# A one-layer hybrid decoder step: the step from the mixers to the feed-forward part, the planner's figures and the rank of the convolutions

## The chip, the cores and the metric

One core of one Trainium2 chip runs the whole kernel. The metric is the device time of one execution in microseconds (us).

## The reference, cut to what matters

2048 prompt tokens and 8 single-token samples pass one decoder layer of width 1024, in fp32:

```python
def trunk_layer(x, ...):
    h = rmsnorm(x, norm_mix_g)
    z = h @ w_in                                   # 1024 -> 1536 columns
    attn_out = sink_attention(q, k, v, ...)        # 8 heads of 64, 2 K/V heads, window 128, ALiBi, sinks
    conv_out = conv_module(z[..., V_END:C_END])    # gated, depthwise over 31 rows, layer norm, silu: 256 channels
    ssm_out  = ssm_module(z[..., C_END:])          # diagonal S5 scan, 16 groups x 64 states, gelu, gate
    x = x + jnp.concatenate([attn_out, conv_out, ssm_out], -1) @ w_out
    hf = rmsnorm(x, norm_ffn_g)
    return x + (silu(hf @ w_ff_gate) * (hf @ w_ff_up)) @ w_ff_down    # 1024 -> 2816 -> 1024
y = rmsnorm(trunk_layer(x), norm_final_g)
```

The new K/V rows, convolution rows and scan states are outputs too.

## The kernel before

**Precision.** Each matrix operand is kept as a high part of the faster fp32r type and a low part (the rest), and a product is three matmuls: high by high, high by low, low by high. A weight or activation is "split" by ScalarE, which writes the high part, and VectorE or GpSimd, which writes the low part by a subtraction.

**The planner.** Nearly all of the program is written as generators (tasks) that `Flow` runs at build time. A task yields what it needs next: an engine, buffers by tag, events. `Flow.run` repeatedly looks for the task that could begin first by an estimated clock for each engine, takes the tasks of the same engine that could begin within `SLACK` ns of it, and issues the piece of the one with the lowest priority number. What comes out is a fixed order of instructions for each engine and for the one DMA queue (SyncE's); on the chip each engine goes through its own order and waits by semaphores. The durations are those of `Engine.cost` (a function of the operation and of its columns), and `Flow.dma`. They are never run: they only choose the order. All instructions carry line 222 (the helper `planned`) and all DMAs line 163, so a trace is read by tile names.

**The mixers (first part).** The tokens are four quarters (512, 512, 512, 520 columns). `w_stream` (priority 50) multiplies each by w_in; `ssm(q)` (1 + q), `conv(q)` (100 + q) and `attention(q)` with its blocks (about 9.5 + 8 q to 17 + 8 q) are the mixers. The convolution is 31 multiply-adds of VectorE over 2 x 512 columns, a step of two at a time between which the planner may place other work. `out_stream` (45) multiplies the mixers' result by w_out, adds the residual and stores x2, in eight units m for each quarter; after a quarter's last unit it forms the inverse norm (two ones-matmuls for quarter 3, a square root on ScalarE, a reciprocal on VectorE), `RS_LATE` = 8000 ns later.

**The feed-forward part (second part).** The columns are three groups g (2 x 344, 2 x 342, 2 x 342 columns), and the intermediate width eleven steps f. A gate or up matrix of a step is a 2 x 2 block product by Strassen's scheme in Winograd's form: seven products of blocks in place of eight. The weights' blocks are A11, S1, S2, A12, S4, S3, A22 (in the order of use, 12 matmuls each), where S1 to S4 are sums that group 0 forms (VectorE, tag `sw`), splits and stores, and that groups 1 and 2 load again. The activations' blocks are B11, T1, T2, B21, B22, T3, T4, in the same order of use. They are formed from x2 by `prep_raw` (stored to DRAM, `hraw`), and loaded and split by `prep_block` through `tx` tiles, of which there are two. For group 0 their split halves lie in the two `h` tiles that the projection uses before (B11, T1, T2 in the first that comes free, B21, T3, T4 in the second, which is free when the projection has ended) and in a tile of its own for B22. `matrix` collects the products in PSUM banks of tag `mm` (three): A11 (bank a), S1 (c), S2 (b), then A12 onto a, S4 onto c, S3 onto b, and A22 into a fourth use of the tag. A bank is freed when VectorE or ScalarE has read its result. PSUM has three more banks of tag `sc` and two of tag `tr`. `down(g)` multiplies the products by w_ff_down and VectorE adds them to eight accumulator tiles `xa`, loaded with x2 by `load_acc`; `final` transposes and normalizes them at the end of a group.

The seam is the place where `out_stream` ends and `gate_up(0)` begins.

Of the kernel before, what the change touches and what calls it, by code (L numbers as in the profile page):

```python
# [9 lines left out]
F32 = mybir.dt.float32  # L10
F32R = mybir.dt.float32r
BF16 = mybir.dt.bfloat16
AF = mybir.ActivationFunctionType
OP = mybir.AluOpType
# [14 lines left out]
W = [512, 512, 512, 520]  # L29
TILES = [[(0, 512)]] * 3 + [[(0, 256), (256, 264)]]  # L30
RS_LATE = 8000.0
C1 = 6.28125
C2 = 0.0019350051879882812
C3 = 3.0199159819567e-07
# [17 lines left out]
class Flow:  # L52
# [89 lines left out]
    def rel(self, tag):  # L142
        self.free[tag].append(self.cur["fin"])
        self.free[tag].sort()
# [31 lines left out]
class Engine:  # L176
# [8 lines left out]
    def cost(self, op, out, ins, args, kw):  # L185
        n = 1
        for d in out.shape[1:]:
            n *= d
        psum = any(x.space == PSUM for x in ins)
        if self.name == "PE":  # L190
            if op == "transpose":
                return max(54.0, args[1].shape[0] / 1.2 + 2.5)
            if ins[0].dtype == F32R:
                return max(123.0, n / 2.4 + 18.0)
            ns = max(215.0, n / 0.6 + 6.0)
            return ns / 2 + 1.0 if out.shape[0] <= 64 else ns
        if self.name == "ACT":
            table, ns = self.TABLE.get(args[2]), 0.0
            if table and table != self.table:
                self.table, ns = table, 1283.0  # L200
            extra = sum(isinstance(kw.get(x), bass.AP) for x in ("scale", "bias", "accum_out"))
            return ns + (51.0 if psum else 94.0) + 94.0 * extra + 0.833 * n
        if self.name == "POOL":
            return 146.0 + (0.85 if op in ("memset", "affine_select") else 2.1) * n
        cols = sum(x.free_size() == 1 for x in ins)
        fast = op in ("tensor_copy", "tensor_scalar") and not psum
        per = 6.25 if op == "reciprocal" else 0.52 if fast else 0.26 if op == "memset" else 1.042
        at, read = (out.tensor, out.offset), [(x.tensor, x.offset) for x in ins]
        dep = 127.0 if self.wrote in read or at in self.read else 0.0
        self.wrote, self.read = at, read  # L210
        return 67.0 + 61.0 * cols + per * n + dep
# [15 lines left out]
def hybrid_step(  # L227
# [9 lines left out]
    nc = tc.nc  # L237
    fl = Flow(nc)
    fl.BIAS = {"DVE": 0, "POOL": -500}
    fl.SLACK = {"PE": 100, "ACT": 150, "DVE": 0, "POOL": 150, "SP": 50}  # L240
    V, S = Engine(fl, "DVE", nc.vector), Engine(fl, "ACT", nc.scalar)
    G, E = Engine(fl, "POOL", nc.gpsimd), Engine(fl, "PE", nc.tensor)
    dma, rel = fl.dma, fl.rel
# [55 lines left out]
    def ps_tr():  # L299
        return psum.tile([P, 512], F32, tag="tr", name="tr", bufs=2)  # L300
# [306 lines left out]
    def conv(q):  # L607
        yield "acc"
        acc = cpool.tile([P, 2, 512], F32, tag="acc", name="acc", bufs=1)
        yield "DVE", cu_ev[q, 0], cu_ev[q, 1], halo_ev[q], small_ev  # L610
        cu = CU[q]
        for i in range(2):
            V.tensor_scalar(acc[:, i, :], cu[:, i, 0:512], taps[:, i, 0:1], fv[:, i:i + 1], op0=OP.mult, op1=OP.add)
        for t in range(1, TAPS):
            for i in range(2):
                V.scalar_tensor_tensor(acc[:, i, :], cu[:, i, t:t + 512], taps[:, i, t:t + 1], acc[:, i, :],
                                       op0=OP.mult, op1=OP.add)
            if t < TAPS - 1:
                yield "DVE"
        cu_done(q)  # L620
        fl.add(layer_norm_gate(acc, 512, q, 0, "acc"), 2.5)
# [647 lines left out]
    segX_ev = Ev(sum(2 * len(x_rows(q)) for q in range(4)))  # L1269
    segA_ev = Ev(4 + 1 + 1)  # L1270
    segB_ev = Ev(5 + 4 + 1 + 1 + 32 + 4)
    attn_ev = Ev(16)
    for q in range(4):
        for k in range(KT):

# [26 lines left out]
    fl.add(w_stream(plan), 50)  # L1302
    for q in range(4):
        fl.add(ssm(q), 1 + q)
        fl.add(conv(q), 100 + q)
    fl.add(conv_tail(), 8)
    fl.add(states_prompt(), 7.5)

# [328 lines left out]
    def out_stream():  # L1637
        for q in range(4):
            yield "stg", Mev[q]
            ssq = stg()  # L1640
            chain = Ev()
            chain.hit(0.0)
            boxes = []
            for m in range(KT):
                ev, box = Ev(), []
                boxes.append((ev, box))
            fl.add(residual(q, 0, *boxes[0]), -600)
            for m in range(KT):
                if m + 1 < KT:
                    fl.add(residual(q, m + 1, *boxes[m + 1]), -400)  # L1650
                st = {"n": nt[q], "chain": chain}
                chain = Ev()

                def evac(ps, c0, n, q=q, m=m, ev=boxes[m][0], box=boxes[m][1], st=st, ssq=ssq, nxt=chain):
                    yield "DVE", ev
                    x2 = box[0]
                    V.tensor_tensor(x2[:, c0:c0 + n], ps[:, :n], x2[:, c0:c0 + n], op=OP.add)
                    rel("mm")
                    st["n"] -= 1
                    if st["n"]:  # L1660
                        return
                    yield "SP"
                    dma(x2_d[m][:, 512 * q:512 * q + W[q]], x2[:, :W[q]])
                    x2_ev[q, m].hit(fl.now())
                    w = W[q]
                    if m == 0:
                        yield "ACT", st["chain"]
                        S.activation(ssq[:, :w], x2[:, :w], AF.Square)
                        rel("x2")
                        segB_ev.hit(fl.now())  # L1670
                    else:
                        yield "ACT", "stg"
                        sq = stg()
                        S.activation(sq[:, :w], x2[:, :w], AF.Square)
                        rel("x2")
                        segB_ev.hit(fl.now())
                        yield "POOL", st["chain"]
                        G.tensor_tensor(ssq[:, :w], ssq[:, :w], sq[:, :w], op=OP.add)
                        rel("stg")
                    nxt.hit(fl.now())  # L1680
                    if m == KT - 1:
                        yield "stg", fl.later(RS_LATE)
                        rs = stg()
                        for c0, n in TILES[q]:
                            yield "PE", "tr"
                            pm = ps_tr()
                            E.matmul(pm[:, :n], ones_c, ssq[:, c0:c0 + n], start=True, stop=True)
                            yield "ACT"
                            S.activation(rs[:, c0:c0 + n], pm[:, :n], AF.Sqrt, scale=256.0 / D, bias=eps)
                            rel("tr")  # L1690
                        rel("stg")
                        yield "DVE"
                        V.reciprocal(rs[:, :w], rs[:, :w])
                        yield "SP"
                        dma(rs_d[:, 512 * q:512 * q + w], rs[:, :w])
                        rel("stg")
                        rs_ev[q].hit(fl.now())
                yield from dense(outs[KT * q + m], M[q], TILES[q], evac, -500)
            rel("h")

# [88 lines left out]
    def prep_block(g, b):  # L1791

        n = GN[g]
        yield ("SP", "tx", raw_ev[g, b], *([prog[g - 1, NFP - 1]] if g else [hb_free[-1, b]]))
        t = tx_tile().rearrange("p (k c) -> p k c", k=4)[:, :, :n]
        dma(t, raw_d[g][:, RAW.index(b), :, :n])
        yield "ACT", hb_free[g - 1, b]
        hi, lo = HB[b][:, 0, :, :n], HB[b][:, 1, :, :n]
        S.activation(hi, t, AF.Copy)
        yield "DVE"  # L1800
        V.tensor_tensor(lo, t, hi.bitcast(F32), op=OP.subtract)
        rel("tx")
        HB_ev[g, b].hit(fl.now())


    SUMS = ["S1", "S2", "S4", "S3"]
# [127 lines left out]
    def matrix(g, f, kind, done):  # L1934
# [27 lines left out]
            V.tensor_tensor(t["p5"], t["p5"], t["u3"], op=OP.add)  # L1962
            fl.add(done(1, 1, t["p5"], "gs", False), -500)

        def c21(ps):
            yield "DVE", e["u3"]
            V.tensor_tensor(t["r"], ps[:, :n], t["u3"], op=OP.add)
            rel("mm")
            rel("stg")
            fl.add(done(1, 0, t["r"], "stg", False), -500)  # L1970

# [22 lines left out]
        rel("whl")  # L1994
        fl.add(plus_r("u3", b, "stg", True), -500)
        fl.add(c22(), -499)
        yield "PE", "mm", u.ready["A22"], HB_ev[g, "T4"]
        d = ps_mm()
        yield from part(d, n, u, "A22", g, "T4", True, f, kind)
        rel("whl")  # L2000
        fl.add(c21(d), -500)

    def gate_up(g):
        n = GN[g]
        for f in range(NFP):
            prog[g, f].hit(fl.now())
            gate, gate_ev = {}, {(i, j): Ev() for i in range(2) for j in range(2)}
# [109 lines left out]

    def load_acc(g, m):

        yield ("SP", "xa", *[x2_ev[q, m] for q in quarters(g)])  # L2120
        x = fpool.tile([P, 688], F32, tag="xa", name="xa", bufs=8)
        dma(x[:, :2 * GN[g]], x2_d[m][:, G0[g]:G0[g] + 2 * GN[g]])
        X[g, m] = x
        X_ev[g, m].hit(fl.now())
# [123 lines left out]
```

## Time and profile before

| | |
|---|---|
| median of 3 runs | 2186.06 us (2183.65 to 2190.08) |
| the profiled execution's own time | 2186.88 us |
| its span, first to last instruction | 2185.1 us |
| TensorE busy | 2091.2 us, 96% |
| VectorE, ScalarE, GpSimd busy | 1533.9, 853.7, 254.0 us |
| granted TensorE clock, mean | 0.987 of full speed |
| DMA | 457.9 MB, 210 GB/s over the span |

The profile is one execution. Engines are called PE (TensorE), DVE (VectorE), ACT (ScalarE), POOL (GpSimd) and SPq (the DMA queue of SyncE); PEld is the weight load, which overlaps PE. A matmul's end is modelled, so "busy" tells that TensorE had work, and not how fast it went.

### The profile page before, as it was taken

What the parts mean: (1) busy time and instruction counts of PE and PEld (TensorE: products, weight loads), DVE (VectorE), ACT (ScalarE), POOL (GpSimd) and SP (SyncE); (2) the same over time, 40 slices, a digit from 0 to 9 for tenths busy, and PEclk for the clock granted to TensorE, in tenths of its full rate; (3) what the DMA queues carried; (4) which work ended last, traced back from release to release, by engine and by line L of the source; (5) the groups of instructions that cost most, each with busy time, mean ns of one, the idle gap of its engine ahead of it and who ended that gap; (6) DMA issues with size and microseconds to landing.
All of it is one profiled execution on the core that took longest, in us unless ns stands there. A gap on an engine that the chain in (4) does not pass through costs nothing.

```text
span 2185.1 us, 35164 instructions
## 1 busy us (share of the span) xinstructions
PE 2091.2 (96%) x13326; PEld 1950.1 (89%) x13326; DVE 1533.9 (70%) x3052; ACT 853.7 (39%) x1682; POOL 254.0 (12%) x183
## 2 busy tenths in 40 slices
PE   8899999999998899999999999999999999999997
PEld 7676777877777899999999999999999999999997
DVE  5998889789954577777787766656656655555555
ACT  6216534777641443333333442222223522222223
POOL 3201110122121322221322000000000000000000
PEclk9999999999999999999999999999999999999998
DMA  8964666688789966655565586656647765554551
GB/s 271 306 226 148 220 200 213 205 234 257 233 296 322 315 228 208 200 202 172 188 217 198 185 267 224 199 166 216 205 145 247 226 202 159 179 164 148 181 158 52
DMA packets 350713, 457.90 MB, mean 210 GB/s; under 512 B 42453, under 2 KB 233760, under 8 KB 340304
## 3 DMA queue, kind: packets, MB, share of 16 engines
q1 hardware_dynamic: 350544, 455.66, 65.0%
q8 instruction: 105, 1.72, 0.3%
q14 instruction: 64, 0.52, 0.1%
HBM read 333.94 MB, written 122.32 MB: 209 GB/s over the span
## 4 chain that ended last, share of the span: by engine, by line
PE 54%; DMA 3%; DVE 2%; issue 1%; ACT 1%; POOL 1%; SPq 0%; DVEq 0%; ACTq 0%; POOLq 0%
PE mm L222 34%; PE sc L222 20%; DMA tx<-hraw 1%; DMA xa<-x 1%; DVE sw L222 1%; POOL whl L222 1%; PE tr L222 1%; ACT whl L222 0%; DMA whl<-sum 0%; ACT h L222 0%; DVE h L222 0%; DVE act L222 0%; DVE gs L222 0%; DVE xa L222 0%; DVE stg L222 0%
## 5 line engine op out<-in xcount | busy, mean ns | idle before, releaser
L222 PE MATMUL mm<-h,whl 128*128 128x342 f32 (+4 forms) x7296 | 1270.3, 330 | 32.9 <-DVE gs L222 8.3
L222 PEld LDWEIGHTS mm<-h,whl 128*128 128x128 f32 x7296 | 1150.2, 190 | 101.4 <-issue 16.7
L222 PE MATMUL sc<-act,whx 128*128 128x342 f32 (+1 forms) x3168 | 514.2, 320 | 5.1 <-DVE xa L222 3.5
L222 PEld LDWEIGHTS sc<-act,whx 128*128 128x128 f32 x3168 | 499.5, 189 | 7.1 <-DVE xa L222 5.1
L222 DVE TENSOR_TENSOR xa<-xa,sc 128x342 f32<-128x342 f32 (+1 forms) x528 | 265.7, 510 | 224.0 <-PE sc L222 211.9
L222 DVE SCALAR_TENSOR_TENSOR acc<-cu,taps,acc 128x512 f32<-128x512 f32 x240 | 173.1, 783 | 0.0
L222 POOL TENSOR_TENSOR whl<-sw,whl 128x512 fp32r<-128x512 f32 x88 | 122.9, 1407 | 331.4 <-ACT whl L222 303.6
L222 ACT ACTIVATE whx<-wraw 128x1024 fp32r<-128x1024 f32 x66 | 66.6, 1053 | 227.7 <-PE sc L222 226.2
L222 PE MATMUL mm<-hb,whl 128*128 128x342 f32 (+1 forms) x792 | 136.0, 320 | 0.0
L222 ACT ACTIVATE stg<-mm 128x342 f32<-128x342 f32 (+3 forms) x100 | 49.8, 498 | 215.9 <-PE mm L222 210.8
L222 PEld LDWEIGHTS mm<-hb,whl 128*128 128x128 f32 x792 | 126.8, 189 | 0.3 <-ACT gs L222 0.3
L222 ACT ACTIVATE whl<-wraw 128x512 fp32r<-128x512 f32 (+1 forms) x122 | 84.9, 696 | 68.2 <-PE mm L222 40.0
L222 DVE TENSOR_TENSOR stg<-mm,stg 128x342 f32<-128x342 f32 (+1 forms) x132 | 67.4, 511 | 48.7 <-PE mm L222 46.3
L222 DVE TENSOR_TENSOR whl<-wraw,whl 128x512 fp32r<-128x512 f32 x102 | 77.8, 763 | 32.8 <-ACT whl L222 32.4
L222 ACT ACTIVATE act<-gs 128x342 fp32r<-128x342 f32 (+1 forms) x99 | 48.1, 485 | 124.4 <-DVE gs L222 124.4
L222 ACT ACTIVATE s<-s,sst 128x256 f32<-128x256 f32 (+1 forms) x196 | 90.3, 488 | 13.3 <-DVE sst L222 13.3
L222 ACT ACTIVATE whl<-xraw 128x512 fp32r<-128x512 f32 x96 | 60.0, 625 | 75.8 <-PE mm L222 36.2
L222 DVE TENSOR_TENSOR whl<-xraw,whl 128x512 fp32r<-128x512 f32 x96 | 74.1, 777 | 14.8 <-ACT whl L222 14.8
L222 ACT ACTIVATE whl<-sw 128x512 fp32r<-128x512 f32 x88 | 52.8, 624 | 78.7 <-PE mm L222 44.7
L222 ACT ACT_TABLE_LOAD x64 | 82.1, 1283 | 3.2 <-issue 1.5
L222 DVE TENSOR_TENSOR whx<-wraw,whx 128x1024 fp32r<-128x1024 f32 x66 | 78.1, 1222 | 3.8 <-ACT whx L222 0.4
L222 DVE TENSOR_TENSOR gs<-mm,gs 128x342 f32<-128x342 f32 (+1 forms) x66 | 33.8, 512 | 61.2 <-PE mm L222 61.2
(232 smaller groups left out, 1854.9 us busy)
## 6 DMA issues: line engine op xcount, KB each, us to landing
whl<-sum SPq DMA_DIRECT2D x176, 512.0 KB
sum<-whl SPq DMA_DIRECT2D x88, 512.0 KB
wraw<-in_w_ff_down SPq DMA_DIRECT2D x66, 512.0 KB
whl<-hl_o SPq DMA_DIRECT2D x24, 1024.0 KB
wraw<-in_w_ff_up SPq DMA_DIRECT2D x44, 512.0 KB
xraw<-in_w_ff_gate SPq DMA_DIRECT2D x42, 512.0 KB
whl<-hl_q SPq DMA_DIRECT2D x12, 1024.0 KB
tx<-hraw SPq DMA_DIRECT2D x14, 684.0 KB
```

Of the source, the lines that this page charges most:

```text
L222: return call(*args, **kw)
```

## The change

The planner's costs: an fp32 matmul of 512 columns into half of the partitions counts 734 ns, a ScalarE operation of over 128 columns with a strided operand 1.7 ns a column, a scan on VectorE 2.2 ns a column. Slack is now 200 ns on VectorE and none on ScalarE and GpSimd. The convolutions' priority is 9 + 8 q, just before the attention of the same quarter. Quarter 3's inverse norm comes 60 us after the projection in place of 8, with both its matmuls ahead of both roots. `gate_up(0)` begins when `out_stream` has ended. Block T4 of group 0 is loaded by four DMAs into four of the five `gs` tiles (`prep_last`) and not through `tx`. A22's product takes a bank of tag `tr` or `mm`, whichever was freed longer ago by the planner's clock. `load_acc` waits for the start of f = 1 of its group.

```diff
-            return ns / 2 + 1.0 if out.shape[0] <= 64 else ns
+            if out.shape[0] <= 64:
+                return 734.0 if n >= 512 else ns / 2 + 1.0
+            return ns
...
-            return ns + (51.0 if psum else 94.0) + 94.0 * extra + 0.833 * n
+            apart = any(x.ap[-1][0] != 1 for x in (out, ins[0])) and n > 128
+            return ns + (51.0 if psum else 94.0) + 94.0 * extra + (1.7 if apart else 0.833) * n
...
-        per = 6.25 if op == "reciprocal" else 0.52 if fast else 0.26 if op == "memset" else 1.042
+        per = 6.25 if op == "reciprocal" else 2.2 if op == "tensor_tensor_scan" else 0.52 if fast else 0.26 if op == "memset" else 1.042
...
-    fl.SLACK = {"PE": 100, "ACT": 150, "DVE": 0, "POOL": 150, "SP": 50}
+    fl.SLACK = {"PE": 100, "ACT": 0, "DVE": 200, "POOL": 0, "SP": 50}
...
-        fl.add(conv(q), 100 + q)
+        fl.add(conv(q), 9 + 8 * q)
...
-                        yield "stg", fl.later(RS_LATE)
+                        yield "stg", fl.later(RS_LATE if q < 3 else RS_LAST)
                         rs = stg()
-                        for c0, n in TILES[q]:
-                            yield "PE", "tr"
-                            pm = ps_tr()
+                        yield ("PE",) + ("tr",) * len(TILES[q])
+                        pms = [ps_tr() for _ in TILES[q]]
+                        for (c0, n), pm in zip(TILES[q], pms):
                             E.matmul(pm[:, :n], ones_c, ssq[:, c0:c0 + n], start=True, stop=True)
-                            yield "ACT"
+                        yield "ACT"
+                        for (c0, n), pm in zip(TILES[q], pms):
                             S.activation(rs[:, c0:c0 + n], pm[:, :n], AF.Sqrt, scale=256.0 / D, bias=eps)
                             rel("tr")
...
             rel("h")
+        out_ev.hit(fl.now())
...
+        if g == 0 and b == "T4":
+            yield from prep_last(n)
+            return
...
+    def prep_last(n):
+
+        yield "SP", "gs", "gs", "gs", "gs", raw_ev[0, "T4"]
+        ts = [gs()[:, :n] for _ in range(4)]
+        for k in range(4):
+            dma(ts[k], raw_d[0][:, RAW.index("T4"), k, :n])
+        yield "ACT", hb_free[-1, "T4"]
+        for k in range(4):
+            S.activation(HB["T4"][:, 0, k, :n], ts[k], AF.Copy)
+        yield "DVE"
+        for k in range(4):
+            V.tensor_tensor(HB["T4"][:, 1, k, :n], ts[k], HB["T4"][:, 0, k, :n].bitcast(F32), op=OP.subtract)
+            rel("gs")
+        HB_ev[0, "T4"].hit(fl.now())
...
-        yield "PE", "mm", u.ready["A22"], HB_ev[g, "T4"]
-        d = ps_mm()
+        bank = min(("tr", "mm"), key=lambda x: fl.free[x][0] if fl.free[x] else 1e18)
+        yield "PE", bank, u.ready["A22"], HB_ev[g, "T4"]
+        d = ps_tr() if bank == "tr" else ps_mm()
...
     def gate_up(g):
         n = GN[g]
+        if g == 0:
+            yield out_ev
...
-        yield ("SP", "xa", *[x2_ev[q, m] for q in quarters(g)])
+        yield ("SP", "xa", prog[g, 1], *[x2_ev[q, m] for q in quarters(g)])
```

## Rows read from the trace of the kernel before

**Rows 1.** Busy time of each engine in stretches, then clock, DMA share, GB/s.
```profile
core 0: us, PE busy (x) PEld busy (x) DVE busy (x) ACT busy (x) POOL busy (x), PEclk, DMA share, GB/s
0.00:360.00 360.00, 326.60 (x2221) 261.01 (x2222) 303.71 (x667) 157.26 (x243) 58.49 (x46) 0.97 0.69 221
360.00:620.00 260.00, 248.47 (x1546) 197.96 (x1545) 231.40 (x695) 183.20 (x502) 45.88 (x30) 0.99 0.77 234
620.00:742.70 122.70, 114.99 (x699) 100.81 (x698) 61.28 (x79) 35.90 (x61) 28.12 (x21) 0.97 0.98 328
742.70:790.00 47.30, 34.49 (x180) 32.70 (x179) 34.07 (x39) 28.11 (x40) 16.86 (x10) 0.86 0.97 328
790.00:1215.00 425.00, 413.75 (x2601) 409.93 (x2600) 324.20 (x512) 150.33 (x275) 104.60 (x76) 1.00 0.59 192
...
1300.00:1650.00 350.00, 350.00 (x2232) 350.00 (x2231) 210.56 (x383) 93.44 (x173) 0.00 (x0) 1.00 0.62 194
```

**Rows 2.** TensorE's timeline in the seam; in brackets idle time before, and who ended it.
```profile
751.16 0.42 PE L222 MATMUL mm<-h,whl 128*128 128x344 f32 x1 [3.20 <-ACT h L222]
752.78 3.34 PE L222 MATMUL mm<-h,whl 128*128 128x344 f32 x11 [1.20 <-DVE h L222]
...
764.42 0.66 PE L222 MATMUL mm<-h,whl 128*128 128x344 f32 x1 [3.87 <-ACT h L222]
766.05 1.80 PE L222 MATMUL mm<-h,whl 128*128 128x344 f32 x5 [0.97 <-DVE h L222]
...
787.20 9.37 PE L222 MATMUL mm<-h,whl 128*128 128x344 f32 x48 [3.58 <-DVE gs L222]
```

**Rows 3.** The DMA queue's timeline in the seam: when loads are issued.
```profile
725.75 1.34 SPq L163 DMA_DIRECT2D tx<-hraw  x2
...
742.92 0.33 SPq L163 DMA_DIRECT2D tx<-hraw  x1
...
756.84 0.38 SPq L163 DMA_DIRECT2D tx<-hraw  x1
757.26 6.08 SPq L163 DMA_DIRECT2D xa<-x  x8
```

**Rows 4.** ScalarE's timeline in the seam.
```profile
765.43 1.28 ACT L222 ACT_TABLE_LOAD   x1
766.72 0.47 ACT L222 ACTIVATE stg<-tr,eps 128x256 f32<-128x256 f32 x1
```

**Rows 5.** ScalarE's groups in 742.7 to 790: busy time, mean ns.
```profile
L222 ACT ACT_TABLE_LOAD x5 | 6.4, 1283 | 0.1
```

**Rows 6.** TensorE's waits in 840 to 1215: in total, times, longest.
```profile
PE mm L222 <- DVE gs L222: 4.7, 4, 1.2
PE mm L222 <- ACT whl L222: 4.3, 6, 0.7
```

**Rows 7.** VectorE's timeline in the seam.
```profile
772.89 3.40 DVE L222 RECIPROCAL stg<-stg 128x520 f32<-128x520 f32 x1 [0.68 <-ACT stg L222]
...
786.64 0.50 DVE L222 TENSOR_TENSOR gs<-mm,gs 128x344 f32<-128x344 f32 x1
```

**Rows 8.** Stretches of 4 us in the seam, columns as in rows 1.
```profile
764.00:768.00 4.00, 2.61 (x7) 2.22 (x8) 2.44 (x2) 3.96 (x6) 3.03 (x2) 0.50 1.01 301
768.00:772.00 4.00, 4.00 (x20) 3.81 (x19) 2.50 (x4) 2.53 (x4) 0.35 (x1) 0.74 1.04 407
...
788.00:792.00 4.00, 4.00 (x20) 4.00 (x19) 3.50 (x7) 0.95 (x2) 0.00 (x0) 0.68 1.05 351
```

**Rows 9.** The chain of waits at the start of group 1.
```profile
1281.46 9.62 DMA xa<-x
```

**Rows 10.** VectorE's timeline: the last taps of quarter 3's convolution.
```profile
608.02 2.71 DVE L222 SCALAR_TENSOR_TENSOR acc<-cu,taps,acc 128x512 f32<-128x512 f32 x4
```

**Rows 11.** TensorE's timeline: the last attention product, and quarter 3's projection.
```profile
614.86 1.94 PE L222 MATMUL tr<-s,vt 128*64 128x512 f32 x8
...
689.55 0.95 PE L222 MATMUL mm<-h,whl 128*128 128x256 f32 x6
```

**Rows 12.** A stretch of the projection, columns as in rows 1.
```profile
630.00:640.00 10.00, 10.00 (x47) 8.11 (x46) 1.93 (x3) 1.74 (x3) 3.04 (x3) 1.00 1.01 323
```

More of the change, by code (lines that the diff above doesn't have):

```diff
@@ L31 @@
 RS_LATE = 8000.0
+RS_LAST = 60000.0
 C1 = 6.28125
@@ L1271, in hybrid_step @@
     segB_ev = Ev(5 + 4 + 1 + 1 + 32 + 4)
-    attn_ev = Ev(16)
+    attn_ev, out_ev = Ev(16), Ev()
     for q in range(4):
@@ L1963, in c22, with c21 @@
             fl.add(done(1, 1, t["p5"], "gs", False), -500)
-        def c21(ps):
+        def c21(ps, bank):
             yield "DVE", e["u3"]
             V.tensor_tensor(t["r"], ps[:, :n], t["u3"], op=OP.add)
-            rel("mm")
+            rel(bank)
             rel("stg")
@@ L1996, in matrix @@
         fl.add(c22(), -499)
-        yield "PE", "mm", u.ready["A22"], HB_ev[g, "T4"]
-        d = ps_mm()
+        bank = min(("tr", "mm"), key=lambda x: fl.free[x][0] if fl.free[x] else 1e18)
+        yield "PE", bank, u.ready["A22"], HB_ev[g, "T4"]
+        d = ps_tr() if bank == "tr" else ps_mm()
         yield from part(d, n, u, "A22", g, "T4", True, f, kind)
         rel("whl")
-        fl.add(c21(d), -500)
+        fl.add(c21(d, bank), -500)
     def gate_up(g):
         n = GN[g]
+        if g == 0:
+            yield out_ev
         for f in range(NFP):
```

## The prediction

> **What bounds the kernel now.** I read the stretches first [rows 1]: busy time of each engine by stage, to see which engine fills which stage. TensorE is the bound nearly everywhere. In groups 1 and 2 of the feed-forward part it is busy 350.00 of 350 us, so nothing there can be won. What is open is its idle time elsewhere: 33.4 us in 0 to 360 (360 less 326.60), 11.5 in 360 to 620, 7.7 in 620 to 742.7, 12.8 in the seam from 742.7 to 790 (where the granted clock is also down to 0.86), and 11.3 in the rest of group 0 (790 to 1215). In 0 to 620 VectorE is the close second: 303.7 of 360 and 231.4 of 260 us.
>
> Then TensorE's timeline in the seam [rows 2], whose brackets tell how long it stood and who let it go. The projection ends near 742.7; group 0's first matrix runs A11, S1 and S2 and stops. It waits for block B21 (3.20 + 1.20 us, the tail of it on VectorE), for block T4 (3.87 for ScalarE's high half, 0.97 for VectorE's low half), and 3.58 us before A11 of f = 1. Third, the DMA queue [rows 3]: the first two blocks' loads go out at 725.75, B21's at 742.92, T4's only at 756.84, just ahead of the eight accumulator loads (xa). Last, the waits of TensorE in the steady part of group 0 [rows 6]: 4.7 us for VectorE's "gs" operations in four places, each before an A11, and 4.3 us for ScalarE's weight halves.
>
> **The change, part by part.** The sum is made against the profiled execution: 2186.88 us, its span 2185.1 and 1.8 around it; it lies 0.8 us over the median 2186.06. The three runs spread over 0.3%, so 0.3% (6.6 us) is about what a measurement here can tell from no change.
>
> *T4 by another way (prep_last).* T4's load no longer waits for a "tx" tile, which the blocks before it free one by one; it takes four "gs" tiles as soon as the raw blocks are in DRAM, by 726, when the first two blocks are loaded [rows 3], and only ScalarE's copy waits for the projection to free the h tile (742.7). Copy and subtraction become four pieces each: a 344-wide piece takes 0.50 us on VectorE [rows 7], and with as much on ScalarE it is 2 us and 2 us. T4 is then ready near 747, and is needed at 760. Its 3.87 + 0.97 = 4.84 us go. B21 keeps its load after 742.9, so its 4.40 us stay: that is what is late next. The gate `out_ev` costs nothing: A11 already runs after the projection's last matmul. The four tiles leave one "gs" for S1's copy, and S2's sum waits for T4's; both are behind B21's wait.
>
> *A22's bank.* With three mm banks, A22 takes the bank that the next A11 could have had, and that A11 waits until VectorE has drained another, at 786.64 to 787.14 in the seam [rows 7]. With A22 in a tr bank A11 finds the first one free. The seam's 3.58 us and group 0's 4.7 [rows 6] go. If S1 then hits the same late bank, up to 1.6 of the 3.58 come back (A11's 12 matmuls at 157 ns are 1.9 us of cover); the next item takes that away.
>
> *The last inverse norm 60 us later.* In the seam ScalarE loads tables five times, 6.4 us [rows 5]; four of these switch to the root and back, twice. VectorE spends 3.40 us on the reciprocal [rows 7], ten microseconds ahead of the drain that A11 waits for. All of it moves to about 805, where one switch and back is left, 2.6 us. There VectorE is busy 76% and ScalarE 35% [rows 1]. If an evacuation queues behind the reciprocal it costs up to 3.4 us, if not nothing; I take 1.5. The result is needed only by group 2.
> ScalarE's root starts 1.29 us after the load before it begins [rows 4], so a switch is 1.28 us here. The Trainium skill, "ScalarE: Activation LUTs", section "What ACT_TABLE_LOAD costs", gives 2.66 us for each switch, with a drain. This row shows no drain; by the page the seam would shed 10.6 us of ScalarE instead of 5.1, and the sum would be the same, since ScalarE is not what TensorE waits for once T4 is early.
>
> *The clock.* After the two stops the granted clock is 0.50 and 0.74 in 764 to 772 and 0.68 in 788 to 792 [rows 8]. At the full level (2.4 GHz) the 2.61 + 4.00 + 4.00 us of matmuls there would take 1.3 + 1.0 + 1.3 = 3.6 us less. Without the stops I count that as won.
>
> *The accumulators (load_acc).* Group 0's eight xa loads leave the seam (128 x 688 words each, 2.82 MB, 8.6 us at the stretch's 328 GB/s [rows 1]) and go out when f = 1 begins. Their cover is the f = 1 gate matrix: 84 matmuls at 157 ns (2232 in 350 us [rows 1]), 13.2 us; in group 1 the same load took 9.62 us [rows 9]. The first is needed first, so nothing is lost; if the queue of weight loads stands before them, up to 3 us. In group 1 these loads go out at 1281 [rows 9], 65 us after the group began, so f = 1 has long started and nothing changes.
>
> *The planner's figures, the slack and the convolutions' place.* These run nothing; they only reorder. The convolutions (240 tap operations of VectorE) move ahead of the attention of their own quarter. Only quarter 3's is moved by much: it runs to 610.7, the last attention product stands at 614.86, and the projection of quarter 3 is in its first unit at 689 [rows 10, 11]. All of that work must be done in 360 to 620 in either order and quarter 3's projection leaves some 75 us of cover, with the projections of quarters 0 to 2 to fill in. I take 0. The bounds are TensorE's idle time there: all 11.5 us won, or as much lost again; the slack of 200 ns on VectorE and none on ScalarE and GpSimd goes with it.
> TensorE's own headroom there is judged by the dense stretch 630 to 640: 47 matmuls in 10.00 us, 213 ns each for 512 columns, at clock 1.00, while weight loads are busy 8.11 [rows 12]. The Trainium skill, "Perfetto Trace Analysis", section "Identifying the Most-Contended Engine", would judge headroom by the busy share of weight loads instead; with 560 of 742.7 us it would leave 183 us to win before the seam. This row is against that here: weight loads at 81% go with a full array.
>
> Sum: 4.84 + 3.58 + 4.7 + 3.6 - 1.5 = 15.2 us. 2186.88 - 15.2 = 2171.7 us, which I give as **2171.5**.
>
> **The rivals.**
> *The seam is bound by DMA (no change).* The DMA engines are 0.97 to 0.98 busy from 620 to 790 [rows 1], and f = 1's weights must come through them. If T4 early only pushes B21 and the weights back, or the xa loads stand before f = 1's weights, the seam's 12 us are waited elsewhere. Left are group 0's 4.7 less 1.5: 2183.7. For it: the busy share. Against: 8.6 us of loads leave the seam, and the first stops end on T4's path, not on weights.
> *VectorE's slack (slower).* Weight halves and sums have the highest rank. With 200 ns of slack they are put before evacuations that are ready sooner; a 512-wide half is some 0.75 us by the 0.50 of 344 [rows 7], a full unit twice that, on an engine busy 60 to 76% in the feed-forward part [rows 1]. One wait of 0.72 us (the size of ScalarE's waits in [rows 6]: 4.3 us in six) in each of 66 matrices is 47.5 us: 2186.9 - 15.2 + 47.5 = 2219; in half of them 2195. It decides from (15.2 + 6.6) / 0.72 = 30 matrices on. Against: a backlog already lets rank decide, and there will be five banks instead of three.
> *The mixers' order (either sign).* The 11.5 us of 360 to 620 won as well: 2160. Or lost: 2183, no change; to be slower than before by 0.3% it would need over 21.8 us, twice the idle time there, as a quarter that stops the projection would.
> *The new ways do nothing:* A22 finds tr banks taken by the last transposes of the group before, and T4's four tiles are refused until the h tile is free. Then only the late norm is left, which at most saves the seam's 3.58 and 1.3 of clock and costs 1.5: 2183.5.
>
> **How the numbers follow.** Forecast 0.60, with the mixers' gain on top 0.07: faster, 0.67. DMA-bound seam 0.12, mixers' loss 0.05, new ways idle 0.03: no change, 0.20. VectorE's slack 0.08, and a mixers' loss of over 21.8 us 0.05: slower, 0.13. The range goes from the forecast with the mixers' 11.5 and the late norm's 1.5 won, 2158, less 2 for the rest of the idle time before 360, 2156, up to the forecast with 11.5 lost there, 3 for xa, 1.9 more for the reciprocal, 2188. That leaves out the slower cases and little else. The likeliest case's own range is 2165 to 2179.
>
> **What would show it.** Right: TensorE's two waits for T4 gone and B21's still there; no root on ScalarE between 742 and 790; A22 written to tr; the waits for "gs" before A11 gone from group 0, which then goes 0.4 us faster per f (4.7 over 11); no clock under 0.9 after 760. Wrong: a new wait of the f = 1 matrices for wraw or xraw loads, of the first down product for xa, waits in groups 1 and 2, or a projection that begins its first matrix of the feed-forward part at another time than 742.7 by more than 12 us: then the mixers' order decides, not the seam.

## The result, and the profile after

| | before | after |
|---|---|---|
| median | 2185.81 us, 4 runs | 2158.00 us, 4 runs (2156.18 to 2161.03) |
| profiled execution, its span | 2186.88, 2185.1 us | 2156.18, 2154.4 us |

The ratio is 0.987, 95% interval 0.9857 to 0.9884: faster by 27.8 us, or 1.3%. The forecast was 2171.5: right in sign and inside its range, but 15.2 us where 27.8 came. The profiled executions lie 30.7 us apart, since the one after is the fastest of its four; what is read from the two traces below adds up to that.

The stretches come first again, cut where the stages lie now (columns as in [rows 1]).

```profile
core 0: us, PE busy (x) PEld busy (x) DVE busy (x) ACT busy (x) POOL busy (x), PEclk, DMA share, GB/s
0.00:360.00 360.00, 336.30 (x2284) 272.16 (x2285) 306.44 (x675) 161.22 (x248) 59.54 (x46) 0.97 0.72 225
360.00:620.00 260.00, 242.62 (x1462) 191.57 (x1462) 229.66 (x680) 179.77 (x480) 49.56 (x33) 0.99 0.77 231
620.00:737.00 117.00, 114.98 (x717) 99.44 (x716) 61.72 (x92) 35.52 (x76) 23.48 (x18) 0.99 1.01 346
737.00:777.00 40.00, 30.82 (x172) 29.99 (x171) 29.81 (x35) 21.71 (x37) 15.19 (x10) 0.87 0.82 265
777.00:1190.00 413.00, 412.72 (x2614) 412.03 (x2613) 331.21 (x519) 152.88 (x281) 105.88 (x78) 1.00 0.64 208
```

Against [rows 1]: group 0 after the seam, 11.3 us idle before, now stands 0.3 of 413. The seam is shorter, but its idle time only fell from 12.8 to 9.2 us and its clock is still 0.87. Before 360 the idle time fell from 33.4 to 23.7 us; from 360 to 620 it rose from 11.5 to 17.4, and from 620 to the end of the projection it fell from 7.7 to 2.0.

To say where the time came from I cut both profiled executions at the same pieces of work: the start of S4 in the gate or up matrix of a step (the only product that reads the tile `hb`, so each is seen in TensorE's timeline). The first stands at 755.9 before and at 749.5 after; A11, the first product of the feed-forward part, begins at 742.1 before and at 737.0 after, so 5.1 us of these 6.4 were won ahead of it.

| from, to (us) | before | after | gain | forecast |
|---|---|---|---|---|
| start, S4 of group 0, f = 0, gate | 755.9 | 749.5 | 6.4 | 0 |
| on to S4 of f = 1, gate | 40.5 | 34.9 | 5.6 | with the next |
| on to S4 of f = 2, gate | 42.9 | 42.5 | 0.4 | 12.0 |
| on to S4 of f = 10, up | 374.8 | 362.1 | 12.7 | 3.2 |
| start of group 1 (to its f = 2, up) | 133.2 | 130.3 | 2.9 | 0 |
| middle of group 1 | 331.7 | 331.7 | 0 | 0 |
| start of group 2 | 133.2 | 130.8 | 2.4 | 0 |

That is 30.4 of the 30.7 us between the spans. (The seam's 12.0 are T4's 4.84, A11's 3.58 and the clock's 3.6; group 0's 3.2 are 4.7 less 1.5.)

TensorE's timeline in the seam, to be laid beside [rows 2]; in brackets the idle time before, and who ended it:

```profile
744.29 5.34 PE L226 MATMUL mm<-h,whl 128*128 128x344 f32 x24 [3.37 <-DVE x L226]
...
752.94 1.99 PE L226 MATMUL mm<-h,whl 128*128 128x344 f32 x11 [1.26 <-DVE h L226]
754.77 2.06 PE L226 MATMUL tr<-h,whl 128*128 128x344 f32 x12
...
763.29 7.93 PE L226 MATMUL mm<-h,whl 128*128 128x344 f32 x36 [4.56 <-DVE gs L226]
...
776.73 3.49 PE L226 MATMUL mm<-h,whl 128*128 128x344 f32 x21
```

A22 writes to `tr` at 754.77 and waits for nothing: T4's 4.84 us are gone. A11 of f = 1 (776.73) waits for nothing: its 3.58 us are gone. B21's wait is gone too. In their place stand two waits for banks and one of 1.26 us for T3's low half (752.94). S2 waits 3.37 us for the evacuation `x<-mm,x` of the projection's last unit, and S1 of the first up matrix waits 4.56 us for the drain of the gate matrix. VectorE's timeline says what stood ahead of these drains:

```profile
740.93 2.87 DVE L226 TENSOR_TENSOR h<-gs,h 128x344 fp32r<-128x344 f32 x4
743.72 0.42 DVE L226 TENSOR_TENSOR x<-mm,x 128x264 f32<-128x264 f32 x1
...
756.24 3.47 DVE L226 TENSOR_TENSOR whl<-wraw,whl 128x512 fp32r<-128x512 f32 x2
761.33 0.69 DVE L226 TENSOR_TENSOR sw<-xraw 128x512 f32<-128x512 f32 x1 [1.63 <-DMA xraw<-in_w_ff_gate]
762.11 0.69 DVE L226 TENSOR_TENSOR sw<-sw,xraw 128x512 f32<-128x512 f32 x1
762.72 0.51 DVE L226 TENSOR_TENSOR gs<-mm,gs 128x344 f32<-128x344 f32 x1
```

T4's four new low halves (2.87 us) stand ahead of the first drain. Ahead of the second stand weight work and a sum for f = 1 that waits for its load. Why that load is late shows in the DMA queue's waits from 740 to 765 (in total, times, longest) and in the stretches (columns as above):

```profile
SPq L164 <- POOL whl L226: 7.4, 2, 6.9
```

```profile
744.00:748.00 4.00, 3.71 (x15) 3.74 (x16) 1.96 (x3) 1.10 (x2) 0.00 (x0) 0.60 1.09 353
748.00:752.00 4.00, 3.67 (x24) 3.39 (x22) 3.35 (x5) 3.08 (x5) 2.37 (x2) 1.00 0.06 19
760.00:764.00 4.00, 0.71 (x2) 0.72 (x3) 2.54 (x5) 0.49 (x1) 0.00 (x0) 0.61 1.07 378
764.00:768.00 4.00, 4.00 (x16) 4.00 (x16) 0.78 (x3) 1.73 (x4) 0.00 (x0) 0.54 0.99 372
```

The queue stood up to 6.9 us behind the store of a weight sum whose low half GpSimd had not yet written; the DMA engines were 6% busy from 748 to 752, and the gate weights of f = 1 were issued behind that store, at 752.39: 2.9 us after the first S4, where before (752.06) it was 3.9 us ahead of it. This is read from the order of the queue; no run moved that store. The same rows show the clock: 0.60 and 0.54 where TensorE starts again after the two long stops, so most of these stretches ran at the lower of the clock's two levels (0.50 of full speed, 1.2 GHz). The 15 and 16 matmuls there take 247 and 250 ns; at the 157 ns of [rows 1] they would take 2.8 us less, so most of the 3.6 us that I had counted as won is spent again.

### The profile page after: what moved, and what is told of

Read it like the earlier page. It is cut to its first block, busy times and chain, and to the rows that moved or that the text cites. A ratio compares the mean times of both kernels' runs of the same rounds, so it can differ in the third digit from the quotient of the medians.

```text
span 2154.4 us, 35203 instructions
## 1 busy us (share of the span) xinstructions
PE 2089.3 (97%) x13326; PEld 1952.4 (91%) x13326; DVE 1539.8 (71%) x3060; ACT 855.2 (40%) x1684; POOL 253.6 (12%) x183
## 4 chain that ended last, share of the span: by engine, by line
PE 59%; DMA 1%; DVE 1%; ACT 0%; issue 0%; DVEq 0%; SPq 0%; ACTq 0%
PE mm L226 32%; PE sc L226 22%; PE tr L226 5%; DMA tx<-hraw 1%; DMA xraw<-in_w_ff_gate 0%; DVE h L226 0%; ACT junkf L226 0%; ACT h L226 0%; DVE act L226 0%; DVE tx L226 0%; DVE y L226 0%; DVE xa L226 0%; DVE whl L226 0%; DVE sw L226 0%; DVE gs L226 0%
## 5 line engine op out<-in xcount | busy, mean ns | idle before, releaser
L226 PE MATMUL mm<-h,whl 128*128 128x342 f32 (+4 forms) x6576 | 1167.9, 332 | 13.7 <-DVE gs L226 4.6
L226 PEld LDWEIGHTS mm<-h,whl 128*128 128x128 f32 x6576 | 1042.5, 191 | 75.6 <-issue 11.5
L226 DVE SCALAR_TENSOR_TENSOR acc<-cu,taps,acc 128x512 f32<-128x512 f32 x240 | 180.1, 814 | 0.1
L226 PE MATMUL tr<-h,whl 128*128 128x342 f32 (+1 forms) x720 | 122.3, 319 | 0.0
L226 PEld LDWEIGHTS tr<-h,whl 128*128 128x128 f32 x720 | 114.5, 188 | 0.0
```

The lines of the kernel that those rows point to most:

```text
L226: return call(*args, **kw)
```

## The experiments

Two theories stood behind them. By the first, group 0's gain is the bank: with A22 in `tr` the three `mm` banks stop running out. By its rival it is the order: the slack, the cost figures and the convolutions' rank decide whether VectorE drains banks in time, here and in the mixers. "After" is the changed kernel; each "all but" kernel is it with one part undone. Ratios are to the kernel before on the same chip (its median 2189.1, 2189.8 and 2189.0 us in the three batches). A part's worth is the difference of ratios times 2186 us, uncertain by some 4 to 6 us. In experiments 1, 4, 5 (with the old slack) and 7 the time that came was named by neither theory.

**1. The bank alone.** The kernel before, with
```diff
+        bank = min(("tr", "mm"), key=lambda x: fl.free[x][0] if fl.free[x] else 1e18)
...
-        d = ps_mm()
+        d = ps_tr() if bank == "tr" else ps_mm()
...
```


> The kernel before with one part of the change: A22's product in a tr bank. Bank theory: the 13.0 us that group 0 lost between its f = 1 and its last step, and the 5.4 us at the starts of groups 1 and 2, all come from the fourth use of three mm banks. Then TensorE is busy over 99% from 850 to 1150 and the time is 2185.8 - 18 - 3 (the wait before A11 of f = 1) = 2165. Rival, order theory: the new slack and the planner's figures put VectorE's work of group 0 in a better order; the bank alone saves the 4.7 us of 'gs' waits and the 3.6 us before f = 1: 2177, and ScalarE's weight-half waits of 0.7 us stay in group 0.


2186.41 us, 0.9987 (0.9977 to 0.9998). From 840 to 1190 all of A11's and S2's waits for a bank are gone. The 5.8 us left there are two waits of another kind, before S3 (the product behind S4): S3 is added onto S2's bank once VectorE has formed a sum from S2's product (`gs<-mm,stg`), and that sum stands late in VectorE's order. From 790 on it is 10.8 us in four places, one before S1 for a bank and three before S3. TensorE's timeline, with VectorE's sum between:
```profile
969.44 2.04 PE L222 MATMUL mm<-hb,whl 128*128 128x344 f32 x12
...
973.52 0.50 DVE L222 TENSOR_TENSOR gs<-mm,stg 128x344 f32<-128x344 f32 x1
...
974.07 3.81 PE L222 MATMUL mm<-h,whl 128*128 128x344 f32 x12 [2.59 <-DVE gs L222]
977.68 3.23 PE L222 MATMUL tr<-h,whl 128*128 128x344 f32 x12
```
So the bank takes the waits for banks away, and by itself it is not enough.

**2. All but the bank.**
```diff
...
-        d = ps_tr() if bank == "tr" else ps_mm()
+        d = ps_mm()
...
```


> The changed kernel with A22 back in an mm bank. Bank theory: group 0 has waits of TensorE at every second step again, and it is 2158 + 18 = 2176. Order theory: only 5 to 8 us come back, 2163 to 2166, and group 0 keeps most of its pace.


2182.93 us, 0.9970 (0.9956 to 0.9984). A11's and S2's waits in group 0 are all back, so the bank is needed: 22 us of the 28 go with it, where alone it gives 3.

**3. The seam's parts and the bank, without the planner's figures, the slack and the rank.** The kernel before, with the diff's `prep_last`, `out_ev`, `RS_LAST` and its loop, `load_acc` and the bank.


> The four seam parts together (T4 through gs tiles with the gate, the late inverse norm, the later accumulator loads, the bank), with the planner's figures, slack and convolution rank of before. Bank theory: all but the mixers' 5 us, 2185.8 - 25 = 2161. Order theory: the seam's 6 us, the 4.7 of 'gs' waits, nothing else: 2175.


2178.28 us, 0.9954 (0.9939 to 0.9968): 10 us. TensorE still stands 4.9 us between 840 and 1190, in two waits before S3 as in experiment 1.

**4. The planner's three alone.**
```diff
+    fl.SLACK = {"PE": 100, "ACT": 0, "DVE": 200, "POOL": 0, "SP": 50}
...
+        fl.add(conv(q), 9 + 8 * q)
```
and the three cost figures.


> Only the planner's figures, the slack and the convolutions' rank, no seam part. Bank theory: the projection ends 5 us earlier and nothing else changes, 2181. Order theory: 5 us in the mixers and some 10 us in group 0, 2171.


2195.88 us, 1.0037 (1.0019 to 1.0054): slower by 8 us. The new order makes long waits from f = 0 to 2, as TensorE's timeline shows: 6.12 us for T4, which goes through `tx` here, 4.19 before S3 for S2's sum, and twice 4.55 before S2 for one of the three banks:
```profile
763.06 0.65 PE L225 MATMUL mm<-h,whl 128*128 128x344 f32 x1 [6.12 <-ACT h L225]
...
783.29 9.37 PE L225 MATMUL mm<-h,whl 128*128 128x344 f32 x48 [4.19 <-DVE gs L225]
797.21 5.56 PE L225 MATMUL mm<-h,whl 128*128 128x344 f32 x24 [4.55 <-DVE stg L225]
...
848.77 5.52 PE L225 MATMUL mm<-h,whl 128*128 128x344 f32 x24 [4.55 <-DVE stg L225]
```
One half of the change is worth 10 us, the other -8, both 28: the parts are not to be added, and neither theory holds by itself.

**5. All but the slack, and half of it.**
```diff
-    fl.SLACK = {"PE": 100, "ACT": 0, "DVE": 200, "POOL": 0, "SP": 50}
+    fl.SLACK = {"PE": 100, "ACT": 150, "DVE": 0, "POOL": 150, "SP": 50}
```


> The changed kernel with the slack of before (VectorE 0, ScalarE and GpSimd 150). Theory: the bank and the slack each free only half of what the other needs; without the slack group 0 has 7 us of waits as with the seam parts alone, and the starts of groups 1 and 2 have 5 us more: 2158 + 12 = 2170. Rival, the planner's figures or the convolutions' rank did it: 2158 to 2161.


2204.39 us, 1.0063 (1.0041 to 1.0086): slower than the kernel before. And with `"DVE": 100`:


> The changed kernel with 100 ns of slack on VectorE in place of 200. If the slack works by letting urgent work go first that is ready a little later, half of it gives most of the gain: 2158 to 2170, mixers within 10 us of the changed kernel's, group 0 clean. If the good order is one of many that a small shift brings about, group 0 has waits of another period and the mixers move by more, in either direction: 2175 or more.


2215.50 us, 1.0128 (1.0113 to 1.0143): half the slack does not give half the gain, it is slower than none. VectorE's timeline at 100, the second halves of quarter 3's convolution input and its first taps:
```profile
592.34 0.42 DVE L226 TENSOR_TENSOR cu<-mm,stg 128x256 f32<-128x256 f32 x1
...
598.46 0.43 DVE L226 TENSOR_TENSOR cu<-mm,stg 128x264 f32<-128x264 f32 x1
...
600.31 1.41 DVE L226 SCALAR_TENSOR_TENSOR acc<-cu,taps,acc 128x512 f32<-128x512 f32 x2
```
and the stretch 360 to 620 of the same kernel, columns as before:
```profile
360.00:620.00 260.00, 226.31 (x1367) 177.00 (x1367) 197.75 (x643) 160.10 (x453) 33.76 (x20) 0.92 0.66 199
```
In the changed kernel that convolution's input is complete at 445.8 and its taps run from 447.0 to 558.5; here they run from 600.3 to 673.5 (without the new slack from 587.9 to 656.9), so VectorE is 32 us less busy in this stretch and TensorE stands 33.7 of 260. The first S4 comes at 803.3 (793.6 without the slack) in place of 749.5. In both, TensorE's timeline has units of the projection in place of quarter 3's last input unit. That the planner took them because they rank ahead of it (45 against 50) is argued, not tried.

**6. All but the convolutions' rank.**
```diff
-        fl.add(conv(q), 9 + 8 * q)
+        fl.add(conv(q), 100 + q)
```


> The changed kernel with the convolutions at priority 100 + q. If their rank is what ends the projection 5 us earlier: 2163, with the first feed-forward matmuls 5 us later. If it is nothing, as the prediction had it: 2158.


2169.33 us, 0.9908 (0.9888 to 0.9929): 8 us are lost. In the profiled execution the first S4 comes at 763.7, 14.2 us later; group 0 stays clean (349.92 of 350 us busy from 840 to 1190).

**7. All but the cost figures.** Three lines of `Engine.cost` as before.


> The changed kernel with the planner's three figures of before. If these give the mixers' 5 us: 2163. If they are nothing: 2158. Either way group 0 keeps its pace, since none of its operations is costed otherwise.


2182.79 us, 0.9974 (0.9959 to 0.9989): 23 us are lost, 12.1 of them before the first S4 (761.6). The way on to S4 of f = 1 is 6.2 us shorter, but the two pieces behind it are 14.9 us longer (47.0 and 372.5 us), though none of the three figures prices an operation there: TensorE stands 9.8 us from 840 to 1190. VectorE's timeline ahead of one of its waits (S3 begins at 1084.51 after 1.91 us):
```profile
1078.92 1.78 DVE L223 TENSOR_TENSOR whl<-xraw,whl 128x512 fp32r<-128x512 f32 x1
1080.62 0.68 DVE L223 TENSOR_TENSOR sw<-xraw,sw 128x512 f32<-128x512 f32 x1
1082.08 1.36 DVE L223 TENSOR_TENSOR whl<-xraw,whl 128x512 fp32r<-128x512 f32 x1 [0.77 <-ACT whl L223]
1083.35 0.68 DVE L223 TENSOR_TENSOR sw<-xraw 128x512 f32<-128x512 f32 x1
1083.96 0.50 DVE L223 TENSOR_TENSOR gs<-mm,stg 128x344 f32<-128x344 f32 x1
```
and the like place of the changed kernel, where S3 (1023.90) does not wait, on both engines:
```profile
1015.45 4.84 PE L226 MATMUL sc<-act,whx 128*128 128x344 f32 x30
1015.65 0.52 DVE L226 TENSOR_TENSOR gs<-mm,stg 128x344 f32<-128x344 f32 x1
...
1022.02 2.04 PE L226 MATMUL mm<-hb,whl 128*128 128x344 f32 x12
1023.90 2.06 PE L226 MATMUL mm<-h,whl 128*128 128x344 f32 x12
```
The same work stands in another order. Here four weight operations, one with a wait of its own, stand ahead of S2's sum (`gs<-mm,stg`), and A12 and S4 follow S2 at once. In the changed kernel VectorE forms that sum as soon as S2 has ended, and 30 matmuls of the down product come before A12. The start of group 1 is 5.3 us longer too (135.6).

**8. All but T4's own way** (`prep_last` taken out, `out_ev` kept).
```diff
-        if g == 0 and b == "T4":
-            yield from prep_last(n)
-            return
```


> The changed kernel with T4 of group 0 loaded through a tx tile as before (the gate before group 0 stays). The prediction's step: T4 late by 4.8 us again, and 2 of clock, 2165. Rival: the seam now waits for banks that VectorE drains late (4.56 us before S1 of the up matrix), so T4 late only moves that wait, 2158 to 2161.


2166.72 us, 0.9898 (0.9876 to 0.9920): 6 us are lost by the ratios, whose intervals just meet; the profiled spans are 10.8 us apart. A22 waits for T4 again, in TensorE's timeline:
```profile
762.51 0.66 PE L226 MATMUL tr<-h,whl 128*128 128x344 f32 x1 [5.71 <-ACT h L226]
764.14 3.52 PE L226 MATMUL tr<-h,whl 128*128 128x344 f32 x11 [0.97 <-DVE h L226]
```
The rival had a part in it: of the 4.56 us before S1 of the up matrix 1.40 are left, but waits of 1.05 before S3 and 2.10 before an A11 come up by 829.

**9. All but the late norm** (`RS_LATE` for every quarter, and the old loop).
```diff
-                        yield "stg", fl.later(RS_LATE if q < 3 else RS_LAST)
+                        yield "stg", fl.later(RS_LATE)
...
```


> The changed kernel with quarter 3's inverse norm 8 us after the projection as before. The prediction's step: two roots with their table loads and the reciprocal of 3.4 us are back in the seam, ahead of the drains; the seam is 3 to 4 us longer, 2161 to 2162, and group 0 is the same. Rival, order: the seam is no worse, but group 0 starts in another order of VectorE's work and keeps 1 to 2 us waits at every second step, 2168 or more.


2162.15 us, 0.9881 (0.9867 to 0.9896): 2 us are lost by the ratios, whose intervals overlap. The traces show 5.6 us more in the seam (40.5 against 34.9) and 0.9 less in f = 1 (41.6 against 42.5).

**10. All but the accumulators' wait.**
```diff
-        yield ("SP", "xa", prog[g, 1], *[x2_ev[q, m] for q in quarters(g)])
+        yield ("SP", "xa", *[x2_ev[q, m] for q in quarters(g)])
```


> The changed kernel with group 0's accumulators loaded as soon as their tiles exist. The prediction's step: nothing, or the 8.6 us of loads in front of the weights of f = 1; with T4 loaded early now these are the next to be late, so the seam is 0 to 5 us longer: 2158 to 2163. Rival, order: group 0 picks up periodic waits as when the planner's figures are those of before, 2170.


2159.10 us, 0.9861 (0.9844 to 0.9877): no difference from the change's 0.987.

**11. The first product in another bank**, to take the 3.37 us wait away.
```diff
+        own = "sc" if g == 0 and f == 0 else "mm"
+        yield "PE", own, u.ready["A11"], HB_ev[g, "B11"]
+        a = ps_sc() if own == "sc" else ps_mm()
...
```


> The changed kernel with one more step: the A11 products of step f = 0 of group 0 collect in an sc bank, idle until the first down product, so that the mm banks are needed one product later. Bank theory of the seam: the 3.4 us before S2 (a bank that the projection's last evacuation frees) go, and of the 4.6 us before S1 of the up matrix 1.9 to 3 go: 2152 to 2154. Rival: VectorE is behind by then, so the next product waits for the same drain, 2157; or group 0's order is disturbed, over 2165.


2159.13 us, 0.9864 (0.9848 to 0.9879): not to be told from the change. That wait is gone and the next ones show, in TensorE's timeline:
```profile
744.33 0.42 PE L226 MATMUL sc<-h,whl 128*128 128x344 f32 x1 [2.82 <-ACT h L226]
745.96 3.30 PE L226 MATMUL sc<-h,whl 128*128 128x344 f32 x11 [1.20 <-DVE h L226]
753.11 2.01 PE L226 MATMUL mm<-h,whl 128*128 128x344 f32 x11 [1.81 <-DVE h L226]
...
774.90 7.48 PE L226 MATMUL mm<-h,whl 128*128 128x344 f32 x36 [2.71 <-DVE gs L226]
```
2.82 and 1.20 are the wait for B21, 1.81 is T3's, and 2.71 is left of the 4.56. S4 of f = 1 comes 2.1 us earlier, less than the runs can tell.

## Why the prediction was right in sign and short in size

**T4's own way: right.** Both of its waits went, and undoing it costs 6 us, give or take as much, where 4.84 and part of the clock's 3.6 were forecast. "T4 is then ready near 747" holds too (its low halves end at 743.8). What I left out is what its four subtractions stand ahead of on VectorE: 2.87 us in front of the drain that S2 needs.

**"B21 keeps its load, so its 4.40 us stay": wrong as put, right as the next wait.** S2 came 3.37 us late by its bank, and B21 was ready behind it; with S2 released (experiment 11) B21's 4.02 us are back.

**The clock's 3.6 us: wrong.** It needed a seam without stops. Waits of 3.37, 1.26 and 4.56 us took the stops' place, and 2.8 of the 3.6 were spent again, with the clock at 0.61 and 0.54 from 760 to 768 where I had said none under 0.9. Of the 12.0 us forecast from the first S4 to f = 2, 6.0 came (the wait of 3.37 lies ahead of that S4). Counted from the start of one matmul to the start of the next, stops there took 10.3 us over the usual 0.157 before and 6.1 after, and other slow intervals, most of them matmuls of 0.287 us at the lower clock, 4.1 and 2.4: 5.9 of the 6.0.

**A22's bank: right in kind, mis-sized most of all.** Group 0 gave 12.7 us where the sum had 4.7 less 1.5. The step that failed is the reading of [rows 6], "4.3 us for ScalarE's weight halves", which I left in place. They were waits for a bank that VectorE drains. All engines at one of these waits in the kernel before (a timeline):
```profile
1094.51 0.50 DVE L222 TENSOR_TENSOR stg<-mm,stg 128x344 f32<-128x344 f32 x1
1094.54 0.63 ACT L222 ACTIVATE whl<-wraw 128x512 fp32r<-128x512 f32 x1 [1.49 <-PE mm L222]
...
1095.15 0.40 PE L222 MATMUL mm<-h,whl 128*128 128x344 f32 x1 [0.70 <-DVE stg L222]
```
S2 begins at 1095.15, 0.14 us after VectorE's drain ended (1095.01), while ScalarE's half runs on to 1095.17 and so can't be what it waited for. At the six places labelled ScalarE the same half ends within 0.02 us of S2's start, the drain 0.15 us before it at all eight, and the view names the later one. Where the releaser is not in doubt, as at T4's halves in [rows 2], TensorE starts 0.05 us after its end. The Trainium skill, "Perfetto Trace Analysis", section "Per-instruction lifecycle: what the profiler-reported window actually captures", says that the semaphore's way to the other engines comes after the end that a profile shows; the drain's 0.15 us agree with that, a half that ends at the start or after it does not. With A22 in `tr` none of these waits, nor of A11's, is left from 840 to 1190 (experiments 1, 3 and 7), and without it they are there (experiments 2 and 4). So 10.4 us of waits went: 4.7 for "gs", 4.3 for "ScalarE" and 1.4 named rightly ([rows 6] did not show those). The rest of the 12.7 is in how a bracket counts: from the modelled end of the last matmul, 0.16 us behind the place where the next would have begun. The matmul ahead of the S2 above began at 1094.14, 1.02 us earlier where 0.157 is usual, and the bracket says 0.70. From start to start the twelve waits cost 12.3 us.

But the gain stayed only because the order made no other wait. With the old order or figures the same bank leaves 5.8, 4.9 and 9.8 us from 840 to 1190, all of it before S3, for S2's sum (experiments 1, 3 and 7), and with the old slack or half of it 5.1 and 6.7 us, in waits before S1, S3 and A11 (experiment 5). With the new slack and figures, and the rank, T4 or the norm undone, nothing is left. My sum had the bank's gain and the order's as separate terms, the second at 0.

**The late norm: right in its cost, its gain left out.** I took 1.5 us of cost; f = 1 shows 0.9. That the seam would be 5.6 us longer without it, as the trace of experiment 9 shows, stands nowhere in the sum as a gain; by the ratios the part is worth 2 us, within the noise. No root is left between 742 and 790; ScalarE's timeline has it here:
```profile
825.85 1.28 ACT L226 ACT_TABLE_LOAD   x1
827.14 0.85 ACT L226 ACTIVATE stg<-tr,eps 128x256 f32<-128x256 f32 x2
```

**load_acc: right,** nothing.

**"I take 0" for the mixers' order: wrong, inside its bounds.** 5.1 us came ahead of A11, and not from 360 to 620, where I looked: TensorE's idle time fell by 9.7 us before 360, for which my range had 2, rose by 5.9 to 620, and fell by 5.7 behind it. Slack, rank and figures are needed together (experiments 5 to 7: 44.1, 14.2 and 12.1 us lost up to the first S4). A quarter 3 whose convolution comes late is the stopped projection that I gave 0.05: experiment 5 is that case.

**"Groups 1 and 2: nothing can be won": wrong by 5.3 us.** I had read 1300 to 1650, their middle. The waits of TensorE from 1190 to 1300 in the kernel before, in total, times, longest:
```profile
PE sc L222 <- DVE xa L222: 1.9, 2, 1.4
PE mm L222 <- ACT stg L222: 0.8, 1, 0.8
```
After there are none. The starts of both groups take 130.0 to 131.5 us in the kernels with the new slack and the new figures, and 131.7 to 134.8 in those with the old slack or half of it. The slack alone does not decide it: with the new slack and the old figures (experiment 7) the start of group 1 takes 135.6 and that of group 2 130.4.

**The rivals.** The DMA-bound seam was not seen: the queue even stood still, though one load of f = 1's weights came late (VectorE waited 1.63 us for it ahead of a drain). The slack's rival has some support in experiment 4, which is 0.37% slower and waits 4.55 us at a time for drains. But experiment 2, with the same slack and as few banks, is not slower than the kernel before; so that "there will be five banks instead of three" is what kept the rival away is argued and not shown. The mixers' loss came with the slack undone.

What stays open: how the planner's choices in the mixers carry over into the order of group 0. The runs show that the slack and the figures are both needed there, and not by what steps.

## What to carry to other kernels

When a trace names a releaser that ended at the very moment of the start, list every engine's operation that ended in the microsecond before, and ask which resource the waiting instruction needs; here the true one ended 0.05 or 0.15 us earlier each time, and at two of eight repeats the label changed. A free bank is worth only what the drains' place in the draining engine's order lets it be worth, so price a buffer and the order of its releaser as one term, and for a greedy planner try a slack at several values, since half of it can be worse than none. When a stop is taken away, list what stands ahead of each drain on VectorE and of each load in the DMA queue: here T4's new subtractions ahead of one drain, and a store ahead of the load that another drain's forerunner needed, put two stops of 7.9 us in all into the seam.

## What the runs showed of the hardware

VectorE's sums of 512 columns take 0.68 to 0.69 us, as at 761.33 above, but about 1.7 us where GpSimd is at work: in the changed kernel GpSimd runs from 749.6 to 759.2, and VectorE's sums at 752.80 and 754.68 take 1.77 and 1.63 us. Over the whole trace of the changed kernel 74 such sums with no GpSimd operation beside them take 0.67 to 0.69 us, and 14 that overlap one take 1.76 at the median. I had priced a half at 0.75. The Trainium skill, "SBUF — State Buffer", section "Terms", says that the two engines share a pair of ports which one holds for a whole instruction while the other is blocked; these rows agree, and no run here took GpSimd's work away to try it.
